# Two weight rows moved behind the later rwkv batches, and a block's input normalised ahead of the last context steps

## The chip, the cores and the metric

The kernel runs on one core of a Trainium2 chip. The metric is the device time of one execution in microseconds (us); less is better.

## The reference, cut to what matters

Two blocks run one after the other on a sequence of 512 tokens of width 1024. The first block (norm, projection, a gated linear recurrence beside dilated attention, output projection) gives `x`. The second block modulates its norms with six vectors that come from a conditioning vector, `mod = silu(c_2) @ w_ada_2 + b_ada_2`, cut into six pieces of 1024. Pieces 0 and 1 modulate the first norm, piece 2 scales the mixer's output, pieces 3 and 4 modulate the second norm, piece 5 scales the mixture of experts:

```python
p_l = modulate(x, norm1_g, mod[0], mod[1]) @ w_in      # 512 latent tokens
p_c = modulate(ctx, norm1_g, mod_c[0], mod_c[1]) @ w_in  # 256 context tokens
...
S_c, y_c = wkv_bidir(S0, *prep_c)      # rwkv over the context, both directions
_,   y_l = wkv_bidir(S_c, *prep_l)     # then over the latent tokens
...
x = x + mod[2] * mix
x = x + mod[5] * hier_moe(modulate(x, norm2_g, mod[3], mod[4]))
```

So the pieces 2 and 5 are needed late: one after the mixer, one inside the experts. The kernel calls the two rows `m2` and `m5`.

## The kernel before, in words

All is in single precision. A large product is split into a high and a low part of each operand and made of three matmuls (`mm3`, lines 311 to 313). A weight chunk of 512 KB is loaded into a raw buffer by SyncE's queue (`load_chunk`, line 298), and copied to its high part by ScalarE (line 305) and its low part by VectorE (line 306).

The program is written as one list of work. Which instruction each engine takes next is fixed when the kernel is built, by a planner that runs through an assumed timeline and, of the instructions that it takes to be ready, picks the one that stands earliest in the list. On the chip every engine, and every DMA queue, then runs its own list strictly in order. To put work into gaps, the list is woven by hand with Python generators: `step(n)` advances the generators of the modulation vectors in `fill` by n steps, and `cstep(n)` those of the context.

One step of `m2` or `m5` (`row_steps`) computes 256 columns of a row. SyncE's queue loads 256 bias values and two weight chunks of 512 KB; TensorE makes eight products of 32 x 256 (16 MATMUL records, line 384); ScalarE copies the sum out of PSUM (line 386); TensorE adds the four partial rows with one small product (two records, line 388); VectorE adds the bias (line 389), for `m2` also a factor (line 391); SyncE's queue stores 1 KB to DRAM (line 392). Four steps are a row, eight are both.

```python
r, b = (t2(name + z, w=256, tag="t1") for z in "rb")
...
p = ps(name + "p", "mm")
...
raw = load_chunk(w, v0 * 1024 + c * 256, kt=4, ..., nw=256, k0=4 * kh)
```

The buffers of a step, that is the two `t1` tiles, the two `mm` banks of PSUM and the raw buffers, belong to groups that the projections of the same stage use too. There are four raw buffers up to the end of the context and two during the rwkv batches; `mm` has three banks before and two after.

The order of the list around the change is this. First block's output, `mix`. Then the context's steps (`ctx_steps`): after a norm and two projections come the twelve steps of `rw_prep` for the context, which are two of low-rank inputs, two of low-rank outputs (line 772), four of keys and four of values (`vt`, lines 727 to 729 and 845); the second half of the keys is finished inside the first step of values (`key2`, lines 811 to 826). Then the four steps of `m2`. Then the second block's input: `norm_rows` (lines 424 to 427) and `mod_T`, which transposes `mix` in eight column blocks (line 436), scales each out of PSUM (lines 449 and 451) and splits it into high and low part (lines 453 and 454); the result is `h2`. Then the four steps of `m5`. Then the pools of weight buffers and of PSUM are closed and new ones are opened in their place, and the latent half begins: `rw_prep` over `h2` with 14 projections, woven with batches 0 to 3, which run the recurrence over the context, and with ten projections for gates. After it the batches 4 to 11 run the recurrence over the latent tokens. A batch loads its keys and decays (`kb`, `kr`, lines 1132 to 1136), makes products, sends a triangular matrix through DRAM (lines 1183 and 1187), inverts it with a long list of small VectorE instructions (`ph_s`, lines 1199 and 1201), sends it back through DRAM (lines 1204 and 1218) and updates the state (`ph_b`). Behind the batches in the list come the projections for queries, keys, values, pooling and the remaining gates of the latent tokens (`pt` and `pf` on TensorE); they need only `h2` and weights, so they run between the batches' instructions.

Of the kernel before, what the change touches and what calls it, by code (L numbers as in the profile page):

```python
# [186 lines left out]
def build(tc, A, out, dbg=None, upto=99):  # L187
    with ExitStack() as ctx:
        _build(ctx, tc, A, out, dbg, upto)


def _build(ctx, tc, A, out, dbg, upto):
# [61 lines left out]
    def t2(name, dt=F32, w=512, tag="t2"):  # L254
        return cur["bp"].tile([128, w], dt, tag=tag, name=name, bufs=NB[tag])
# [26 lines left out]
    def cc(name):  # L282
        g, o, w = _COFF[name]
        return csts[g][:, o:o + w]
# [67 lines left out]
    def step(n=1):  # L352

        while n and fill:
            try:
                next(fill[0])
                n -= 1
            except StopIteration:
                fill.pop(0)
# [98 lines left out]
    def hl(src, name, w=512):  # L458

        h = t2(name + "h", F32R, w)  # L460
        l = t2(name + "l", F32R, w)
        SC.activation(h, src, AF.Copy)
        V.tensor_tensor(l, src, h.bitcast(F32), ALU.subtract)
        return h, l
# [171 lines left out]


    yb = []
    MX = 4
    MS, MA = (0, 0, 0, 4), (3, 2)  # L640
    bias1 = cc("bias1")
    def att_scores(ft, e):

# [241 lines left out]
    def ctx_steps():  # L885

        xc = []
        for i in range(2):
            t = t2("xc%d" % i, w=1024, tag="t4")
            with tc.issue_after(ld1):  # L890
                SY.dma_start(t, A["ctx"][128 * i:128 * (i + 1), :])
            xc.append(t)
        hcH = bp.tile([128, 8, C], F32R, name="hcH")
        hcL = bp.tile([128, 8, C], F32R, name="hcL")
        norm_rows(xc, "hc")
        hc = mod_T(xc, gsc, sh2[:, 8:16], "hc", lambda f: (hcH[:, f], hcL[:, f]))
        yield
        kc = tok_tiles(W2, 1024, "kc", hc, 2)
        yield
        for i, t in enumerate(kc):  # L900
            qk_norm(t, "kcn")
            V.tensor_tensor(t.rearrange("p (h r) -> p h r", r=64), t.rearrange("p (h r) -> p h r", r=64),
                            qkg[:, None, 64:128].to_broadcast([128, 8, 64]), ALU.mult)
            dump("kc", t, 128 * i)
        for f, o in enumerate(to_feat(kc, "kcT", 2)):
            h, l = hl(o[:, :C], "kcs", C)
            spill_k(f, h, l, slice(512, 768))
        vc = tok_tiles(W2, 1536, "vc", hc, 2)
        for i in range(2):
            SY.dma_start(vcd2[:, i, :], vc[i])  # L910
        yield
        yield from rw_prep(hc, C, 0, False, "aux")

    NC = (2, 0, 99)
    cx = ctx_steps()

    def cstep(n=1):
        for _ in range(n):
            next(cx, None)
# [122 lines left out]
    for f in range(8):  # L1042
        src, g = (ya[f], vv("norm_rec")[:, f:f + 1]) if f < 4 else (yb[f - 4], vv("norm_att")[:, f - 4:f - 3])
        V.tensor_scalar(src, src, g, None, op0=ALU.mult)
        yhl.append(hl(src, "y%d" % f))
    cstep(NC[0])
    mix = [t2("mix%d" % i, w=1024, tag="t4") for i in range(4)]
    for cch in range(4):
        hh = halves(A["w_out"], 256 * cch)
        for i in range(4):  # L1050
# [8 lines left out]
            V.scalar_tensor_tensor(m, pa[:, 256:512], rb[:, i:i + 1], m, op0=ALU.mult, op1=ALU.add)  # L1059
    cstep(NC[1])  # L1060
    step(MS[2])
# [15 lines left out]

    cstep(NC[2])
    step(MS[3])
# [3 lines left out]
    cstep(99)  # L1083
    step(MX)

# [21 lines left out]
    def w1(name, shape=(4, 64), bufs=1, dt=F32):  # L1107
        p = rp if name == "AZ" else rpa if name in EARLY else rpb
        return p.tile([128] + list(shape), dt, tag=name, name=name, bufs=bufs)

    def bc(ap, sh):
        return ap.to_broadcast(sh)
# [65 lines left out]
    def ph_i(d, AMB, bi):  # L1178

        for e in range(2):  # L1180
            for i in range(2):
                r0 = 64 * e + 32 * i
                SY.dma_start(atD[bi][e, i].rearrange("q s t -> s q t"),
                             AMB[r0:r0 + 32, e, :, :, 32 * i:32 * i + 32].rearrange("p s f t -> p (s f) t"))
        LT = w1("LT", (32, 32), 2)
        for g in range(4):
            SY.dma_start(LT[32 * g:32 * g + 32].rearrange("p s t -> p (s t)"),
                         atD[bi].rearrange("e i q s t -> (e i q) (s t)"))
        return LT

    def ph_s(d, LT, bi):

        T = w1("Ti", (8, 32), 2)
        SY.dma_start(T.rearrange("p j t -> p (j t)"), A["tinit"])
        tmp = w1("Tm", (8, 32))
        for s in (range(31) if d == 0 else range(31, 0, -1)):
            js, ts_ = (slice(0, s // 4 + 1), slice(s + 1, 32)) if d == 0 else (slice(s // 4, 8), slice(0, s))
            nj, n = js.stop - js.start, ts_.stop - ts_.start
            V.tensor_tensor(tmp[:, :nj, :n], bc(LT[:, s, None, ts_], [128, nj, n]),  # L1199
                            bc(T[:, js, s:s + 1], [128, nj, n]), ALU.mult)  # L1200
            V.tensor_tensor(T[:, js, ts_], T[:, js, ts_], tmp[:, :nj, :n], ALU.add)  # L1201
        td = ttD[bi].rearrange("e i q (j g) t -> g (e i q) j t", g=4)
        for g in range(4):
            SY.dma_start(td[g], T[32 * g:32 * g + 32])
# [122 lines left out]
    def run_b():  # L1327
        n, sts = pend.pop(0)
        ph_b(*sts)
        if n == 3 and dbg is not None and "S_c" in dbg:  # L1330
            for d_ in range(2):
                for e, rows in par:
                    SY.dma_start(dbg["S_c"][128 * d_:128 * d_ + 128][rows, 256 * e:256 * e + 256],
                                 SI[d_, e][rows].rearrange("p a b -> p (a b)"))

    def batch(n):
        d, chs = batches[n]
        AMB = w1("AMB", (2, 2, 4, 192), 3)
        sts = {c - min(chs): ph_a(d, c, c - min(chs), AMB) for c in chs}
        LT = ph_i(d, AMB, n % 4)  # L1340
        while loops:
            ph_s(*loops.pop(0))
        loops.append((d, LT, n % 4))
        pend.append((n, (d, chs, sts, AMB, n % 4)))
        if len(pend) > 2:
            run_b()
# [42 lines left out]
        GP.memset(t, 0.0)  # L1389
    for n in range(4, 12):  # L1390
        batch(n)
    ph_s(*loops.pop(0))
    while pend:
        run_b()
# [744 lines left out]
```

## Time and profile before

| what | value |
|---|---|
| time, median of 3 runs | 1863.11 us (1859.43 to 1864.79) |
| the profiled execution's own time | 1868.35 us |
| its span in the profile | 1866.5 us |
| TensorE busy | 1715.4 us, 92% of the span |
| VectorE busy | 1068.7 us, 57% |
| ScalarE busy | 617.4 us, 33% |
| mean granted TensorE clock | 0.952 of full speed |

A share of the span is a mean over stages with different limits, so the rows below go stage by stage. Times in the rows are microseconds from the span's start. The 1.85 us between the span and the execution's own time lie outside the profile.

### The profile page before, as it was taken

To read this page: it belongs to the slowest core of one execution; us is meant where nothing else is said; L and a number is where in the kernel's file an instruction comes from. 1 tells how busy PE (TensorE), PEld (TensorE's weight loads), DVE (VectorE), ACT (ScalarE), POOL (GpSimd) and SP (SyncE) were. 2 spreads that over 40 slices of the span, in tenths; PEclk is the share of its full clock that TensorE was granted. 3 is DMA by queue.
4 is the path that set the end of the run, shared out by engine and by line. 5 is a ranking of instruction groups with operands and counts; after the bars stand their busy time and mean duration, and the time that the engine had idled before them with its cause. 6 is when DMAs were issued, how large, how long until landed. Compare 5 with 4: busy or idle time off the path is not lost.

```text
span 1866.5 us, 31358 instructions
## 1 busy us (share of the span) xinstructions
PE 1715.4 (92%) x12309; PEld 1216.4 (65%) x12310; DVE 1068.7 (57%) x2489; ACT 617.4 (33%) x1154; POOL 230.4 (12%) x254
## 2 busy tenths in 40 slices
PE   5899998977998899999999969989799999999998
PEld 3884577964665777888888846779644544444444
DVE  3545577374578856989888538865513333432332
ACT  4324555453443232344333324542311111111010
POOL 0110003001104102212200015100100001010100
PEclk8999999987898998999999989999899999999999
DMA  8335723467847555556654367628189999999997
GB/s 295 126 110 198 237 79 124 160 213 210 232 130 183 158 171 126 157 166 157 181 142 122 102 225 240 223 67 311 46 302 387 386 386 386 387 387 387 386 386 275
DMA packets 277744, 417.34 MB, mean 224 GB/s; under 512 B 105788, under 2 KB 128856, under 8 KB 277336
## 3 DMA queue, kind: packets, MB, share of 16 engines
q1 hardware_dynamic: 248696, 384.88, 61.7%
q10 hardware_dynamic: 25568, 16.78, 2.9%
q0 software_dynamic: 3328, 13.63, 2.6%
q8 instruction: 98, 1.61, 0.4%
q14 instruction: 54, 0.44, 0.1%
HBM read 371.70 MB, written 43.53 MB: 222 GB/s over the span
## 4 chain that ended last, share of the span: by engine, by line
PE 73%; DVE 11%; DMA 7%; ACT 3%; issue 3%; SPq 2%; POOL 1%; ACTq 0%; DVEq 0%; POOLq 0%
PE ped L1983 7%; PE peg L1944 6%; PE peu L1951 6%; PE pf L311 5%; PE pf L313 4%; PE pf L312 4%; PE pcb L2015 3%; PE po L1806 2%; PE pt L311 2%; PE pt L313 2%; PE pt L312 2%; PE pg L1917 2%; PE pg L1918 2%; DVE Tm L1199 1%; DMA kb<-kbD 1%
## 5 line engine op out<-in xcount | busy, mean ns | idle before, releaser
L306 DVE TENSOR_TENSOR wl<-wr,wh 128x1024 fp32r<-128x1024 f32 x125 | 153.5, 1228 | 65.0 <-ACT wh L305 63.4
L305 ACT ACTIVATE wh<-wr 128x1024 fp32r<-128x1024 f32 x125 | 131.8, 1056 | 171.5 <-PE pf L312 91.9
L311 PE MATMUL pf<-h2h,wh 128*128 128x512 f32 x344 | 144.5, 420 | 10.7 <-ACT wh L305 4.7
L312 PE MATMUL pf<-h2l,wh 128*128 128x512 f32 x344 | 142.4, 414 | 0.0
L313 PE MATMUL pf<-h2h,wl 128*128 128x512 f32 x344 | 141.2, 410 | 0.0
L1983 PE MATMUL ped<-wd,hid 128*64 128x512 f32 (+1 forms) x528 | 127.6, 585 | 0.7 <-ACT hid L1967 0.7
L1944 PE MATMUL peg<-wg,hTg 128*64 128x512 f32 x512 | 127.0, 597 | 0.0
L1951 PE MATMUL peu<-wu,hTg 128*64 128x512 f32 x512 | 125.1, 594 | 0.0
L2016 DVE TENSOR_TENSOR acc<-acc,pcb 128x512 f32<-128x512 f32 (+1 forms) x124 | 75.9, 665 | 47.0 <-PE pcb L2015 46.8
L1989 POOL TENSOR_TENSOR yl<-ey,yh 128x512 fp32r<-128x512 f32 x30 | 38.3, 1278 | 468.1 <-ACT yh L1988 468.1
L1199 DVE TENSOR_TENSOR Tm<-LT,Ti 128x60 f32<-128x60 f32 (+24 forms) x372 | 86.3, 232 | 14.0 <-DMA LT<-atD 5.3
L1201 DVE TENSOR_TENSOR Ti<-Ti,Tm 128x60 f32<-128x60 f32 (+24 forms) x372 | 82.2, 221 | 8.6
L1951 PEld LDWEIGHTS peu<-wu,hTg 128*64 128x64 f32 x512 | 43.8, 137 | 65.2 <-issue 62.8
L311 PEld LDWEIGHTS pf<-h2h,wh 128*128 128x128 f32 x344 | 67.5, 196 | 28.8 <-ACT wh L305 5.2
L1983 PEld LDWEIGHTS ped<-wd,hid 128*64 128x64 f32 x528 | 39.4, 136 | 71.4 <-issue 67.7
L1944 PEld LDWEIGHTS peg<-wg,hTg 128*64 128x64 f32 x512 | 41.8, 137 | 60.9 <-issue 58.1
L313 PEld LDWEIGHTS pf<-h2h,wl 128*128 128x128 f32 x344 | 66.8, 194 | 21.9 <-issue 5.6
L312 PEld LDWEIGHTS pf<-h2l,wh 128*128 128x128 f32 x344 | 67.3, 196 | 17.7 <-issue 3.0
L1988 ACT ACTIVATE yh<-ey 128x512 fp32r<-128x512 f32 x30 | 18.9, 630 | 166.7 <-DVE ey L1987 94.4
L1921 ACT ACTIVATE hTg<-pg,sh,gs 128x128 f32<-128x128 f32 x64 | 28.2, 456 | 121.7 <-PE peu L1951 55.4
L1924 DVE TENSOR_SCALAR hTg<-pg,gs,sh 128x128 f32<-128x128 f32 x64 | 25.3, 409 | 75.3 <-PE peu L1951 38.4
L311 PE MATMUL pt<-wh,h1h 128*128 128x256 f32 x192 | 56.4, 296 | 6.7 <-ACT q L547 4.3
(958 smaller groups left out, 4309.4 us busy)
## 6 DMA issues: line engine op xcount, KB each, us to landing
wg<-in_w_exp_gate_dram SPq DMA_DIRECT2D x64, 1024.0 KB
wu<-in_w_exp_up_dram SPq DMA_DIRECT2D x64, 1024.0 KB
wd<-in_w_exp_down_dram SPq DMA_DIRECT2D x62, 1024.0 KB
wr<-in_w_in_dram SPq DMA_DIRECT2D x97, 512.0 KB
kb<-kbD SPq DMA_DIRECT2D x24, 384.0 KB
wr<-in_w_out_dram SPq DMA_DIRECT2D x16, 512.0 KB
LT<-atD SPq DMA_DIRECT2D x48, 128.0 KB
thD<-mth ACTq DMA_DIRECT2D x24, 256.0 KB
```

The source lines that it names most:

```text
L305: SC.activation(hi, raw, AF.Copy)
L306: V.tensor_tensor(lo, raw, hi.bitcast(F32), ALU.subtract)
L311: PE.matmul(p, ah, bh, start=start, stop=False)
L312: PE.matmul(p, ah, bl, start=False, stop=False)
L313: PE.matmul(p, al, bh, start=False, stop=stop)
L1199: V.tensor_tensor(tmp[:, :nj, :n], bc(LT[:, s, None, ts_], [128, nj, n]), bc(T[:, js, s:s + 1], [128, nj, n]), ALU.mult)
L1201: V.tensor_tensor(T[:, js, ts_], T[:, js, ts_], tmp[:, :nj, :n], ALU.add)
L1944: mm = PE.matmul(pg[64 * a:64 * a + 64, :], hT[:, k, 64 * a:64 * a + 64], gp[a][k // 4][:, k % 4, :], start=(k == 0), stop=(k == 7), tile_ ...
L1951: PE.matmul(pu[64 * a:64 * a + 64, :], hT[:, k, 64 * a:64 * a + 64], up[a][k // 4][:, k % 4, :], start=(k == 0), stop=(k == 7), tile_posit ...
L1983: PE.matmul(pd[64 * a:64 * a + 64, :], hid[:, m * k + 64 * a:m * k + 64 * a + 64], dn[q][a][:, k, 0:q1 - q0], start=(k == 0), stop=(k == 3 ...
L2015: PE.matmul(p, ohT[R, 128 * i:128 * (i + 1)], yy[R, qs], start=(z == 0), stop=(z == len(parts) - 1))
L2016: V.tensor_tensor(acc[i][:, qs], acc[i][:, qs], p, ALU.add)
```

## The change

The context's steps ahead of the second block's input are cut from all twelve to nine: both low-rank pairs, the four keys, and the first value step with the second half of the keys. `norm_rows` and `mod_T` come next in the list, then the three remaining value steps. The eight steps of `m2` and `m5` are taken out of their two places around the second block's input, and one is put behind each of the batches 4 to 11.

```diff
     yb = []
-    MX = 4
-    MS, MA = (0, 0, 0, 4), (3, 2)
+    MX = 0
+    MS, MA = (0, 0, 0, 0), (3, 2)
     bias1 = cc("bias1")
...
-    NC = (2, 0, 99)
+    NC = (2, 0, 9)
     cx = ctx_steps()
...
     for n in range(4, 12):
         batch(n)
+        step(1)
     ph_s(*loops.pop(0))
```

`MS[3]` is the number of row steps ahead of `norm_rows` and `MX` that behind `mod_T`; `NC[2]` is the number of context steps ahead of `norm_rows`, and a `cstep(99)` behind `mod_T` takes what is left.

## Rows read from the trace of the kernel before

**Rows 1.** Stretches: busy us (instructions) by engine, granted clock, DMA share, GB/s.

```profile
128.00:218.00 90.00, 89.89 (x600) 39.42 (x600) 45.40 (x142) 42.26 (x121) 0.00 (x0) 1.00 0.67 228
392.00:434.00 42.00, 34.20 (x195) 28.28 (x195) 25.68 (x38) 24.32 (x42) 4.96 (x4) 0.88 0.51 133
434.00:469.00 35.00, 22.05 (x175) 8.76 (x175) 16.10 (x32) 12.75 (x26) 5.31 (x10) 0.77 0.82 261
700.00:1088.00 388.00, 368.57 (x4221) 313.41 (x4220) 307.94 (x973) 142.91 (x277) 61.63 (x94) 0.96 0.56 150
1082.00:1101.00 19.00, 3.13 (x34) 2.29 (x34) 3.04 (x8) 1.95 (x4) 0.92 (x1) 0.66 0.77 275
```

**Rows 2.** The chain of waits, 434 to 470: start, duration, what.

```profile
438.91 5.62 DMA m2w2r<-in_w_ada_dram
...
463.12 4.63 DMA wr<-in_w_in_dram
...
467.78 1.06 ACT wh L305
...
468.89 0.79 PE pf L311
```

**Rows 3.** Timeline of TensorE, 398 to 460: start, duration, what, idle before.

```profile
398.49 1.04 PE L436 MATMUL h2T<-cst,mix 128*128 128x128 f32 x8
...
432.44 0.28 PE L313 MATMUL pf<-hcH,wl 128*128 128x256 f32 x1
...
435.48 1.34 PE L384 MATMUL m2p<-m2w0r,st 128*32 128x256 f32 x16
...
452.69 0.59 PE L388 MATMUL m5q<-m5r,cst 128*1 128x256 f32 x2 [0.50 <-ACT m5r L386]
453.60 0.64 PE L384 MATMUL m5p<-m5w1r,st 128*32 128x256 f32 x8 [0.31 <-DMA m5w1r<-in_w_ada_dram]
...
457.44 1.08 PE L384 MATMUL m5p<-m5w2r,st 128*32 128x256 f32 x8 [0.37 <-DMA m5w2r<-in_w_ada_dram]
```

**Rows 4.** Timeline of SyncE's queue, the last spill of the context's keys.

```profile
436.44 1.44 SPq L778 DMA_DIRECT2D kbD<-tha  x2
```

**Rows 5.** Timeline of VectorE, 434 to 456.

```profile
434.07 0.53 DVE L825 TENSOR_SCALAR tha<-tha,ka 128x512 f32<-128x512 f32 x1
...
439.51 0.48 DVE L729 SCALAR_TENSOR_TENSOR vt<-pf,vec,vt 128x255 f32<-128x255 f32 x1
...
440.99 0.79 DVE L451 TENSOR_SCALAR h<-h2T,gs,sh 128x512 f32<-128x512 f32 x1
...
454.82 0.67 DVE L454 TENSOR_TENSOR h2l<-h,h2h 128x512 fp32r<-128x512 f32 x1
```

**Rows 6.** Groups by line, 434 to 469: count, busy us, mean ns, idle before.

```profile
L454 DVE TENSOR_TENSOR h2l<-h,h2h 128x512 fp32r<-128x512 f32 x8 | 5.2, 673 | 0.0
L453 ACT ACTIVATE h2h<-h 128x512 fp32r<-128x512 f32 x8 | 4.9, 627 | 1.7 <-DMA vTD<-vTs 1.7
L451 DVE TENSOR_SCALAR h<-h2T,gs,sh 128x512 f32<-128x512 f32 x4 | 3.2, 800 | 2.0 <-PE h2T L436 2.0
```

**Rows 7.** First and last of 20 like steps behind attention: ns, first and last start.

```profile
L336 PE MATMUL m2scp<-m2scw0r,st x16: 379/379/403, 128.0 to 128.7; 128*32 128x256 f32 x16
...
L336 PE MATMUL m3shp<-m3shw3r,st x16: 379/391/403, 214.7 to 217.2; 128*32 128x256 f32 x16
```

**Rows 8.** The chain of waits, two `kb` loads.

```profile
488.86 6.61 DMA kb<-kbD
...
534.37 3.52 DMA kb<-kbD
```

**Rows 9.** Stretches of those two loads, columns as in the first group.

```profile
488.80:495.80 7.00, 7.00 (x41) 4.88 (x40) 0.24 (x2) 1.94 (x5) 0.10 (x1) 1.00 0.77 206
534.30:538.00 3.70, 3.70 (x17) 2.98 (x16) 2.49 (x8) 1.72 (x5) 0.61 (x2) 1.00 0.65 200
```

**Rows 10.** Waits of SyncE's queue, 700 to 1090: us in total, times, longest.

```profile
SPq L1321 <- ACT yt L1320: 50.9, 9, 23.8
```

## The prediction

> **What bounds the kernel now.** I read the table of stretches first [rows 1], then the chain of waits through the place where work is taken out [rows 2], and then the lists of the single engines there [rows 3 to 6]. The reader is to see two very different stretches. From 434 to 469, where the rows `m2` and `m5` and the second block's input lie, TensorE shows 22.05 us of records in 35 us, at a granted clock of 0.77, that is partly at the lower of its two levels, while the DMA engines are at 0.82 and move 261 GB/s. From 700 to 1088, where the batches 4 to 11 run, TensorE is busy for 368.57 of 388 us at a clock of 0.96, and the DMA engines are at 0.56.
>
> The chain of waits says what the first stretch waits for: weight chunks of the row steps, 5.62 us for one of them, then the first chunk of the latent half, issued at 463.12, which lands 4.63 us later, and its split [rows 2]. The first latent product starts at 468.89. The last product of the context started at 432.44 [rows 3]. So for 36.45 us TensorE does no projection: sixteen chunks of 512 KB, 8.4 MB, pass through raw buffers, and the latent half's first chunk stands behind them in SyncE's queue. That wait ends last in this stretch, and it is a wait for transfers, not for an engine.
>
> **Part 1: the rows leave the stretch.** The step from 36.45 us to what must remain goes by what is late next. Without the rows, the first latent product needs a chunk, its split, and the first column block of `h2`.
>
> The chunk: SyncE's queue still has the context's spills to issue, the last at 436.44 for 1.44 us, so it is free at 437.88 [rows 4]. If the load goes out then, it lands after the 4.63 us measured for the same load, at 442.51; ScalarE's 1.06 us of split end at 443.57 [rows 2], and the first product starts there, as it follows the split's end within a microsecond today. It gains 468.89 - 443.6 = 25.3 us. If the planner issues the load ahead of the spills, the chunk is no limit and the product can start where the context's products end, at about 433: a gain of at most 36 us.
>
> The input: the first two blocks' transposes run at 398.49 [rows 3], but VectorE scales the first block only at 440.99, behind the last value step's instruction at 439.51, and writes the last low part at 455.49 [rows 5]. With three value steps put behind it in the list, its place is behind the end of the second half of the keys, at 434.60 [rows 5]. Its work is 8 x 0.673 + 4 x 0.800 = 8.6 us on VectorE, and 8 x 0.627 = 5.0 us on ScalarE plus the other four scalings [rows 6], so some 9 us if it runs without the rows' instructions between, and it is done at about 444. A projection takes the eight blocks in order, so it can start with the first. The other bound is that the tail stays as it is, first block at 441, last at 455.5: then the first projection can't run through before that, starts in effect at about 450, and gains 19 us. I take 25.3, since chunk and input agree on it, with 19 and 36 as bounds.
>
> **Part 2: three value steps behind the input.** They are the same instructions in another place. Their evacuations, two instructions of 0.48 us on VectorE for each [rows 5], fall beside the first latent projection instead of before the input. TensorE has 42 - 34.2 = 7.8 us without a record from 392 to 434 [rows 1], where the remaining 24 transposes can go; at 1.04 us for eight [rows 3] they are 3.1 us. I cost this edit at nothing; if that cover is gone, the transposes stay where they are and cost their 3.1 us, which lies inside the bounds above. The values' spills come later in their queue by that, and only a batch that updates the state waits for them.
>
> **Part 3: the rows come back behind the batches.** Per step TensorE needs its 16 records, 1.34 us when nothing holds them up, of which the last one's 0.38 us [rows 7] overlap what follows, and 0.59 us for the two that add the partial rows [rows 3]: 0.96 + 0.59 = 1.55 us, and 8 x 1.55 = 12.4 us. ScalarE and VectorE get one or two copies or sums of 256 columns a step, on engines that are busy for 142.91 and 307.94 of the 388 us, and the DMA engines have 44% free there [rows 1]. SyncE's queue gets three loads and a store a step. I cost these at nothing; what it costs if the queue gives no cover is the first rival.
>
> The lower bound is nothing: TensorE lacks 388 - 368.57 = 19.4 us of being busy there, and behind the last batch, where its output goes out to DRAM and in again, 19 - 3.1 = 15.9 us are empty that displaced projections could fill [rows 1]. The upper bound is the pace of the steps today, where they run alone: from 453.60 to 457.44, 3.84 us a step [rows 3], 30.7 us for eight. The nearest row for steps that lie behind other work is attention: 20 like steps ran from 128 to 218 [rows 7], and TensorE was busy for 89.89 of those 90 us [rows 1]. Steps cost their own TensorE time there and no idle time. So I take 12.4 us.
>
> **The sum.** The profiled execution took 1868.35 us, span 1866.5 and 1.85 around it, which is 5.2 us above the median of the three runs. 1868.35 - 25.3 + 12.4 = 1855.4; against the median, 1863.1 - 12.9 = 1850.2 us. Everything after the latent half moves forward with it: the experts' weights at the end are loaded at a rate that the change doesn't touch.
>
> **A rule that speaks against it.** In the trace two loads of `kb` that stand on the chain took 6.61 and 3.52 us [rows 8], the slower one in a stretch where the DMA engines were at 0.77, the other at 0.65 [rows 9]. The Trainium skill, "DMA: Bandwidth & Descriptors", section "Issuing engines are not separate DMA queues", says that all DMAs run on the same 16 engines and interleave, whoever started them. By that rule the batches' small transfers would get slower while a row's chunks are in flight, and the two rows above agree with it in direction. What it would cost is the first rival.
>
> **The rivals.**
> *Late transfers on the batches' path (slower).* The eight steps issue 16 chunks, 8 bias loads and 8 stores on the queue that also issues `kb`, `kr` and the triangular matrices' way through DRAM. A store waits at its head for VectorE's sum, and a chunk for a raw buffer; behind it stand the next batch's loads, and ScalarE, VectorE and TensorE wait for those. Such waits exist: 50.9 us over nine stores of the batches, the longest 23.8 us [rows 10]. Priced at the difference of the two `kb` loads, 3.1 us for each of eight batches, it is 24.7 us: 1863.1 - 25.3 + 12.4 + 24.7 = 1875 us. It makes the change slower from (25.3 - 12.4 + 5.6) / 8 = 2.3 us a batch. Against it: two batches are always in hand ahead of the one that updates the state, and the steps need nothing of the batch that they follow, so they may run early.
> *The input holds the latent half (no difference).* If the tail of `h2` stays at 441 to 455.5, 19 us are gained; if the steps also take 2 us each rather than 1.55, because they hold both `mm` banks while ScalarE and VectorE are busy, 16 to 19 us are lost again: 1860 to 1863 us. For it speaks that the first block lay in PSUM for some 41 us, from 399.5 to 440.99 [rows 3, 5], so something other than its input held it.
> *The rows are hidden (faster still).* If they fill the idle time in the batches and the empty wait behind them, the second term is nothing: 1863.1 - 25.3 = 1838 us, and with the product's start at 433, 1827. For it speak the 19.4 and 15.9 us; against it that the first is made of pieces of a microsecond or two.
>
> **How the numbers follow.** I give the forecast 0.48, late transfers 0.18, no difference 0.14, hidden rows 0.20. The forecast's own range, with the gain from 19 to 29 and the rows from 5 to 16 us, is 1843 to 1858. No change can be told from a measurement here within 0.3%, 5.6 us, so faster is the forecast and the hidden rows, 0.68; the same 0.14; slower 0.18. The range reaches from 1835, which leaves out a third of the hidden rows' case, to 1868, which leaves out most of the late transfers' case: about 2 in 10 together.
>
> **What would show it.** Right: the first latent product near 443 instead of 468.89 and no line 384 before it; the first block of `h2` scaled before 437; the rows' line 384 only after about 670, its steps 1 to 2 us of TensorE each, with the batches' end near 1088 - 25 + 12 = 1075. Wrong: a latent start later than 455, with VectorE or ScalarE of `mod_T` as its last wait; steps in a run with TensorE idle for chunks between them and the projections for queries starting late; or batches that wait for `kb`, the triangular matrices or the store of a row. Any of the last adds to the stretch of the batches, which I have taken as bounded by TensorE; if it is bounded by VectorE's list, the rows are free and the time is under 1843.

## The result, and the profile after

The changed kernel takes 1878.1 us (median of 9 runs, 1871.36 to 1883.98) against 1864.79 us (9 runs) before: the ratio is 1.0071, with an interval of 1.0055 to 1.0087. It is slower by some 13 us, where 1850 and a faster kernel were forecast. The profiled execution has a span of 1876.4 us. The two profiled executions differ ahead of all that the change moves in the list: the first block's output projection starts at 325.0 us before and at 321.6 after. So 3.4 us of each lead below are not the change's, and each delay is larger by as much.

The front part gained about what was forecast. These stretches have the columns of [rows 1]:

```profile
434.00:446.00 12.00, 2.43 (x13) 1.48 (x13) 10.28 (x18) 8.52 (x15) 3.84 (x9) 0.61 0.71 213
446.00:469.00 23.00, 23.00 (x101) 15.98 (x102) 13.29 (x32) 9.62 (x20) 4.26 (x11) 0.91 0.77 226
700.00:1088.00 388.00, 357.92 (x3949) 299.19 (x3949) 285.80 (x907) 131.00 (x257) 50.56 (x82) 0.88 0.58 161
1063.00:1082.00 19.00, 19.00 (x81) 14.79 (x80) 8.67 (x10) 5.22 (x7) 0.14 (x2) 1.00 0.61 196
```

From 446 on TensorE is saturated, where it was waiting for row chunks before. The first latent product and the first scaling of `h2`, from the timelines of TensorE and VectorE:

```profile
439.04 0.66 PE L845 MATMUL vTp<-cst,vt 128*128 128x128 f32 x2 [3.51 <-DVE vt L729]
443.30 0.66 PE L845 MATMUL vTp<-cst,vt 128*128 128x128 f32 x2 [3.60 <-DVE vt L729]
445.98 0.66 PE L845 MATMUL vTp<-cst,vt 128*128 128x128 f32 x2 [2.03 <-DVE vt L729]
446.29 0.78 PE L311 MATMUL pf<-h2h,wh 128*128 128x512 f32 x1
```
```profile
430.42 0.80 DVE L451 TENSOR_SCALAR h<-h2T,gs,sh 128x512 f32<-128x512 f32 x1
```

446.29 instead of 468.89 is a lead of 22.6 us, 19.2 of them the change's. At the latent half's gate (the `tanh` of line 875) it is 700.3 - 667.8 = 32.5 us, 29.1 of them the change's. The loss lies behind that. The projections' first products (line 311), by stretch: busy us and count on TensorE, the same for weight loads, granted clock, DMA share, GB/s. Before:

```profile
680.00:725.00 45.00, 9.27 (x24) 4.93 (x25) 0.86 0.40 123
725.00:770.00 45.00, 14.34 (x40) 8.30 (x40) 0.95 0.66 160
770.00:812.00 42.00, 13.32 (x42) 7.90 (x42) 1.00 0.59 152
```

After:

```profile
680.00:725.00 45.00, 0.00 (x0) 0.00 (x0) 0.68 0.71 177
725.00:770.00 45.00, 0.00 (x0) 0.00 (x0) 0.58 0.43 115
770.00:812.00 42.00, 0.00 (x0) 0.00 (x0) 0.74 0.48 146
812.00:850.00 38.00, 9.93 (x31) 6.67 (x31) 0.91 0.45 130
```

For 132 us no projection runs at all: 106 such products of line 311 in the kernel before, none after. The query projections start at 812.5 instead of 717.2, right behind the last row step. In their place stand the batches' small products and the eight row steps, whose line 384 spreads from 682.9 to 806.7, some 16 us a step. The batches don't get faster by it. Their last `yt` is at 1060.0 instead of 1087.7, a lead of 27.7 us, but it was 32.5 us at the gate: from there they take 392.2 us instead of 387.4, though no projection stands among them for 132 us. VectorE waits for their triangular matrices in that stretch (680 to 810; us in total, times, longest), 11.2 us where it was 2.0 us before (680 to 812):

```profile
DVE Tm L1199 <- DMA LT<-atD: 11.2, 3, 4.5
```

The projections are left over. They fill the wait behind the batches that was empty (19.00 us busy of 19 from 1063 to 1082, 3.13 of 19 in [rows 1]), and still the last gate is at 1139.2 instead of 1118.8. Half of these 20.4 us come back behind the gate: products of the latent attention that stood behind it before now run ahead of it, and from the gate to the experts TensorE has 197.15 us of records instead of 206.32. The experts start 10.4 us late, at 1363.0 instead of 1352.6, and so does everything behind. With the 3.4 us from the front that is 13.8 us, about the 13.3 us between the medians.

Why a step takes 16 us shows where the last two meet. TensorE, then SyncE's queue (start, duration, what):

```profile
779.88 1.43 PE L384 MATMUL m5p<-m5w2r,st 128*32 128x256 f32 x5
...
799.71 0.64 PE L384 MATMUL m5p<-m5w2r,st 128*32 128x256 f32 x8
```
```profile
778.63 1.05 SPq L298 DMA_DIRECT2D m5w2r<-in_w_ada_dram  x1
...
783.98 0.35 SPq L298 DMA_DIRECT2D m5w3r<-in_w_ada_dram  x1
793.73 0.34 SPq L1134 DMA_DIRECT2D kr<-kkD  x1
...
800.41 0.34 SPq L298 DMA_DIRECT2D m5w3r<-in_w_ada_dram  x1
...
803.71 1.44 SPq L298 DMA_DIRECT2D wr<-in_w_in_dram  x1
```

The second half of step 7 runs 21 us after its chunk was issued, because batch work stands before it in TensorE's list. Only then is its raw buffer free for the last chunk (800.41), and the first chunk for the projections comes behind that (803.71). The queue itself also stood from 784 to 793.73 for a batch's `kr`, which waits for VectorE to let go of its buffer; the waits of the queue, 680 to 810 (us in total, times, longest), show this as the largest:

```profile
SPq L1134 <- DVE AR L1154: 15.0, 3, 9.4
SPq L298 <- PE m2p L384: 9.5, 2, 8.3
```

### The profile page after: what moved, and what is told of

It is laid out like the page before. It is cut to its first block, busy times and chain, and to the rows that moved or that the text cites. A ratio compares the mean times of both kernels' runs of the same rounds, so it can differ in the third digit from the quotient of the medians.

```text
span 1876.4 us, 31396 instructions
## 1 busy us (share of the span) xinstructions
PE 1732.9 (92%) x12309; PEld 1230.6 (66%) x12310; DVE 1070.4 (57%) x2489; ACT 617.5 (33%) x1154; POOL 226.5 (12%) x254
## 4 chain that ended last, share of the span: by engine, by line
PE 71%; DVE 13%; DMA 8%; issue 2%; ACT 2%; SPq 2%; POOL 1%; DVEq 0%; ACTq 0%; POOLq 0%
PE ped L1984 6%; PE peg L1945 6%; PE peu L1952 6%; PE pf L311 4%; PE pf L312 4%; PE pf L313 4%; PE pcb L2016 3%; PE po L1807 2%; PE pt L311 2%; PE pt L313 2%; PE pt L312 2%; PE pg L1918 2%; PE pW L1287 2%; DVE wl L306 2%; PE pg L1919 2%
## 5 line engine op out<-in xcount | busy, mean ns | idle before, releaser
L1201 DVE TENSOR_TENSOR Ti<-Ti,Tm 128x60 f32<-128x60 f32 (+24 forms) x372 | 86.0, 231 | 8.9
L1925 DVE TENSOR_SCALAR hTg<-pg,gs,sh 128x128 f32<-128x128 f32 x64 | 25.3, 408 | 75.5 <-PE peu L1952 38.4
```

## The experiments

Ratios and medians are against the kernel before, run on the same chip beside them; its median was 1861.8 to 1864.1 us.

### The two halves of the change, and the rows elsewhere

**The input's new place alone**, rows where they were:

```diff
-    MX = 0
-    MS, MA = (0, 0, 0, 0), (3, 2)
+    MX = 4
+    MS, MA = (0, 0, 0, 4), (3, 2)
...
         batch(n)
-        step(1)
```

> One part alone: nine context steps ahead of the second block's input, the rows where they were before the change. Theories A, B and C agree: the row chunks again stand ahead of the latent half's first chunk, so the first latent product stays within 460 to 470 and the time within 1858 to 1868 us. If the input's place gave the lead by itself, it would be under 1850 us.

Measured: 1851.28 us, 0.9931 [0.9914, 0.9947]. With nine context steps ahead of them, the four steps of `m2` run at 403.8 to 426.6, in the context's gaps, and the first latent product is at 461.75. So 1864.06 - 1851.28 = 12.8 us of gain come without taking the rows out at all. The first product stands where the theories had it, the time lies under their 1858 to 1868.

**The rows' new place alone**, all context steps ahead of the input:

```diff
-    NC = (2, 0, 9)
+    NC = (2, 0, 99)
```

> The other part alone: all context steps ahead of the input as before the change, the rows behind the batches. If the rows' leaving gives the lead, the first latent product starts at 445 to 452, with 17 to 24 us gained there, and the loss behind the batches is the same as in the changed kernel, about 45 us: 1885 to 1893 us. If the place of the input gives the lead, the first product stays near 465 and the time is above 1895 us.

Measured: 1877.7 us, 1.0073 [1.0049, 1.0097], the same as both together and under the 1885 to 1893 expected: first latent product at 445.0, query products only from 810.4. So the rows' leaving gives the lead at the first latent product by itself, and the input's new place adds nothing that the time shows once the rows are gone. The loss belongs to the rows.

**The rows behind the batches' end**, where `FM` brings them up in the pooling's part of the list:

```diff
         batch(n)
-        step(1)
```

> The changed kernel without the step behind each batch; the eight row steps then run where the list still has steps left, in the pooling projections, behind the projections for queries, keys and values. Theory A (the sixteen row chunks stand in the list ahead of the latent projections' chunks and use the same two raw buffers, so TensorE has no projection from about 680 to 812): the lead of 32 us that the changed kernel has at the start of the batches stays, less some 12 us of TensorE work for the rows at the end, so 1840 to 1850 us, first latent query product near 690. Theory B (row transfers and row instructions burden whatever they lie beside): the rows cost as much beside the pooling, 1865 to 1880 us. Theory C (the two mm banks of PSUM or the t1 tiles that a step holds keep the projections away): the pooling projections use the same banks, so at least half the loss comes back, 1855 to 1870 us.

Measured: 1860.86 us, 0.9986 [0.9966, 1.0006]. The query products start at 681.8, the batches end at 1040.8, 47 us ahead of before; then the steps run from 980 to 1084 and hold up the pooling, TensorE is busy for 34.24 of the 50 us from 1050 to 1100, and the last gate is at 1119.6, as before. The lead is lost in another place. The time is in the range of theory C, the start of the query products where theory A had it; what the steps hold back there was not taken apart.

### What holds the projections back

**Their own raw buffers** (256 KB pieces through the two `tp` tiles):

```diff
-                raw = load_chunk(w, ..., kt=4, name=name + "w%d" % c, nw=256, k0=4 * kh)
                 for g in range(4):
+                    if g % 2 == 0:
+                        rt = t2(name + "w", w=544, tag="tp")
...
```

> The changed kernel with the rows' chunks loaded in halves of 256 KB into the two buffers that the pooling uses later, instead of the projections' raw buffers; place, number of bytes, PSUM banks and t1 tiles as in the changed kernel. Theory A: latent query products start near 690 instead of 812, and the time falls to 1845 to 1860 us. Theory B: same bytes, same instructions, no change, 1875 to 1885 us. Theory C: the banks and tiles are as before, no change, 1873 to 1882 us, query products still after 790.

Measured: 1901.09 us, 1.0206 [1.0183, 1.023]: worse, which none of the three theories had. The one that the shared raw buffers alone hold the projections falls here. The first query chunk was split by 661.66, ScalarE's last line 305 before the stop, and still its product waited for the last row step. From the timelines of ScalarE and TensorE:

```profile
660.60 1.06 ACT L305 ACTIVATE wh<-wr 128x1024 fp32r<-128x1024 f32 x1 [1.70 <-PE pf L312]
```
```profile
844.31 0.59 PE L391 MATMUL m5q<-m5r,cst 128*1 128x256 f32 x2 [0.48 <-ACT m5r L389]
844.83 0.39 PE L311 MATMUL pt<-wh,h2h 128*128 128x256 f32 x1
```

**Their sums in other banks of PSUM**, raw buffers shared:

```diff
-            p = ps(name + "p", "mm")
+            p = ps(name + "p", "aux")
...
-            q = ps(name + "q", "mm")
+            q = ps(name + "q", "aux")
```

> The changed kernel, but the partial sums of a row step and their total are taken from the three aux banks of PSUM instead of the two mm banks that the projections use; chunks still pass through the shared raw buffers. Theory banks (banks are given out in the order of the list, so the query projections that stand behind all eight steps get no mm bank before the last step has one): the first query product moves from 812 to before 725; as chunks of later steps still stand ahead of the projections' chunks in the raw buffers, only the chunks that are already split can be used early, so the time falls by 5 to 15 us, to 1863 to 1873. Theory raw buffers (refuted alone by the run with its own raw tiles, but kept here): first query product stays at 800 or later, time 1873 to 1885. Theory loads on the batches' path: no difference, 1873 to 1885.

Measured: 1921.08 us, 1.0312 [1.0275, 1.0348]. Query products start only at 937.0: the raw buffers hold them now, and the steps take some 33 us each. The theory of the raw buffers had the late start, none of the three the time. The `aux` banks are those of the batches' own updates; that sharing them sets this pace was not tried by itself.

**Both** of these edits:

> The changed kernel with both: the steps' sums in the aux banks, and their weights as 256 KB pieces through the two large tp tiles instead of the projections' raw buffers. A step then holds nothing that the projections use. Theory banks: the query products start at 680 to 720 and fill the batches as in the kernel before, and the gain in front is kept: 1843 to 1860. Theory turns (the steps' pieces among the batches' instructions set the pace by themselves, not what they hold): the batches end later than 1060 and the time stays at 1873 to 1900. Theory loads (the 8.4 MB slow the batches' own transfers): batches' end later than 1065, 1865 to 1880.

Measured: 1897.6 us, 1.0208 [1.0174, 1.0242]. The time is in the range of the theory of turns, but its sign did not come: the batches end at 1002.0, not after 1060. Now the first sixteen query products start at 685.4, and from 725 to 900 there is nothing of line 311. What they wait for is the third group that a step takes from: the `t1` tiles. The first user of `t1` behind the rows is the copy `sw` for the queries' tables, and the first sum `dq` is taken out of PSUM right behind the last row's copy. VectorE's `sw` (duration, first and last start), then ScalarE's timeline:

```profile
L1410 DVE COPY sw<-qkg x1: 222/222/222, 916.3 to 916.3; 128x128 f32<-128x128 f32 x1
```
```profile
916.72 0.36 ACT L389 ACTIVATE m5r<-m5p 128x256 f32<-128x256 f32 x1
916.99 0.37 ACT L1456 ACTIVATE dq<-pt 128x256 f32<-128x256 f32 x1
```

**Nothing shared with the next projections:** sums in `aux`, row and bias in one `tp` tile, weights in 128 KB pieces through the halves of the other:

```diff
-            r, b = (t2(name + z, w=256, tag="t1") for z in "rb")
+            r, b = ROW[0][:, 0:256], ROW[0][:, 256:512]
...
+                    raw = ROW[1][:, 256 * (g % 2):256 * (g % 2) + 256]
+                    SY.dma_start(raw, w[2 * (4 * v0 + c) + kh][:, 256 * g:256 * g + 256])
```

> The changed kernel, its row steps with nothing that the projections use: sums in the aux banks, row and bias in one of the two large tp tiles, weights in pieces of 128 KB through the halves of the other. Theory list order (every shared group of buffers, the raw buffers, the two mm banks and the six t1 tiles, is handed out in the order of the list; with raw buffers and banks taken away, the queries' first sum still waited from 691 until 917 for its t1 tile, behind the last row step): query products run from 690 on without a gap and fill the batches; the gain in front is kept, and the rows cost 0 to 15 us: 1840 to 1862. Theory that the loads or the turns of the steps among the batches' instructions cost the time in any case: query products may start early, but the batches end after 1080 or the projections run at half their pace, 1870 to 1900.

Measured: 1889.02 us, 1.0133 [1.0097, 1.0169]. The start came as the theory of the list's order said. Time and batches' end (1111.2) came as the other theory said, that loads or turns cost the time in any case. `sw` is at 696.1 and the first query sum at 697.1:

```profile
L1409 DVE COPY sw<-qkg x1: 214/214/214, 696.1 to 696.1; 128x128 f32<-128x128 f32 x1
```

But the `tp` tiles belong to the pooling, which comes later, and the steps last until 1040. ScalarE's timeline shows the same picture one group further:

```profile
1039.83 0.38 ACT L387 ACTIVATE row<-m5p 128x256 f32<-128x256 f32 x1 [1.26 <-PE m5p L385]
1040.11 0.59 ACT L1510 ACTIVATE plu<-pf 128x512 f32<-128x512 f32 x1
```

### What the loads cost, and what the holding

**Without the sixteen loads**, banks and `t1` shared:

```diff
-                raw = load_chunk(w, ..., kt=4, name=name + "w%d" % c, nw=256, k0=4 * kh)
-                    PE.matmul(p[...], st[:, 4 * kh + g, :], raw[:, g, :],
+                    PE.matmul(p[...], st[:, 4 * kh + g, :], H2[4 * kh + g][0].bitcast(F32)[:, 0:256],
```

> The changed kernel without the sixteen loads of the row steps' chunks: their products read blocks of h2 instead, so the contents of the rows m2 and m5 are not the weights' and the output differs. Sums stay in the mm banks. Theory banks: the steps keep their pace of 10 us or more, as each stands at its place in the list behind its batch, and the query products still start only when the last step has its banks, after 780: 1865 to 1880. Theory loads: steps shrink to 2 to 4 us of elapsed time each, the query products start before 725, and the time falls to 1838 to 1855.

**The same with nothing held** (sums in `aux`, row and bias in a `tp` tile):

> The same without the loads of the rows' weights: products read blocks of h2, so the contents of the rows m2 and m5 are not the weights' and the output differs; sums in the aux banks, row and bias in a tp tile. Beside the run without loads that shared banks and t1 tiles (1856), it prices what holding these two costs alone. Theory list order: query products from 690, 1832 to 1850, at least 6 us under 1856. Theory loads alone (banks and tiles cost nothing once the steps don't wait for transfers): the same as 1856 within 4 us.

Measured: 1856.08 us, 0.9978 [0.9952, 1.0004], and 1831.05 us, 0.983 [0.9797, 0.9863]. Without loads the steps pass in 66 us (681 to 747) and the query products start at 752.6; both figures lie between the two theories of this run. With nothing held that the projections take next they start at 686.4, and the steps take from 696 to 970 to pass, which no longer shows in the time. Line 311 in that run:

```profile
680.00:725.00 45.00, 10.43 (x32) 6.87 (x32) 0.91 0.59 139
725.00:770.00 45.00, 13.95 (x42) 7.89 (x42) 1.00 0.65 173
770.00:812.00 42.00, 11.18 (x33) 6.02 (x32) 1.00 0.52 152
```

107 products where the changed kernel had none. Taken away in this order, the loads are worth 1878.1 - 1856.1 = 22 us and the holding that is left without them 25 us. The two do not simply add. With the holding taken away first and the loads kept, which is the run with nothing shared, the time is 1889.0, and leaving the loads out gains 1889.0 - 1831.1 = 58 us from there. That run passes its weights in 128 KB pieces through one small tile, so the 58 us are not the price of the transfers alone.

**All eight steps ahead of batch 4**, and **four behind batch 4, four behind batch 5**, everything shared:

```diff
+    step(8)
     for n in range(4, 12):
         batch(n)
-        step(1)
```

> All eight row steps in a run ahead of batch 4 in the list, behind the latent half's gate, instead of one behind each of the batches 4 to 11; banks and raw buffers shared as in the changed kernel. Theory banks: the banks are free for the query products as soon as the steps are through, at the 3.8 us a step of the kernel before after some 31 us, so the first query product comes at 700 to 735, and the time is 1850 to 1866. Theory turns or loads: the eight steps cost the same wherever they stand, first query product after 780, 1872 to 1890.

> The changed kernel with four row steps behind batch 4 and four behind batch 5 in the list instead of one behind each of eight batches; everything shared as in the changed kernel. Theory list order: the time follows the moment when the last row step lets go of its t1 tiles and the queries' first sum is taken out of PSUM. From the runs so far: let go at 692, 755, 760, 825 and 848 us gave 1831, 1858, 1856, 1878 and 1901, some 0.4 us for each us. Here between the run with all eight ahead of batch 4 (755) and the changed kernel (825): 760 to 800, and 1858 to 1872. Theory that the price is of the transfers alone: the same as the changed kernel, 1873 to 1885.

Measured: 1857.99 us, 0.9981 [0.9961, 1.0001], and 1862.69 us, 1.0009 [0.9987, 1.003]. Both times lie where the theory of the banks, or of the list's order, put them. With all eight ahead of batch 4 the query products start at 747.1, though, later than the 700 to 735 expected: in a run there the steps take some 9 us each, not 3.8. The first query sum is taken out at 754.8 and 762.4. In order of that moment:

| run | first `dq`, us | time, us |
|---|---|---|
| nothing held, no loads | 692.5 | 1831.1 |
| all first | 754.8 | 1858.0 |
| no loads | 760.3 | 1856.1 |
| four by four | 762.4 | 1862.7 |
| the change | 825.0 | 1878.1 |
| own raw buffers | 848.0 | 1901.1 |
| other banks and own raw buffers | 917.0 | 1897.6 |
| other banks | 941.5 | 1921.1 |

That is (1921.1 - 1831.1) / (941.5 - 692.5) = 0.36 us for each us of delay. It is a trend over different kernels, not a law; the rows' new place alone (820.9, 1877.7) lies on it, the run with nothing shared (697.1, 1889.0) lies off it: its pooling waited until 1040, and its batches ended at 1111.2, against 1052.9 without the loads. So does the run with the rows behind the batches' end (687.8, 1860.9), whose loss comes later.

### The row that the forecast used

**m2 in the first block's attention**, m5 ahead of the input, and **all eight there**, with `(0, 0, 0, 0), (4, 3)`; the input's new place kept, no step behind the batches:

```diff
-    MS, MA = (0, 0, 0, 0), (3, 2)
+    MS, MA = (0, 0, 0, 4), (4, 2)
```

> The input's new place kept; the four steps of m2 are woven into the first block's attention (four steps after each even head instead of three), the four of m5 stand behind the nine context steps ahead of the input, none behind the batches. Theory that a step among saturated work costs its own TensorE time where what it holds is not shared with work in waiting: attention grows by 4 x 1.55 = 6 us, the m5 steps run in the context's gaps at 400 to 430 plus 6, the first latent product stands 10 to 16 us earlier relative to that than in the run with the input's place alone (461.8): 1836 to 1850. Theory that what counts is only the rows' transfers wherever they are: no better than 1851.

> All eight row steps in the first block's attention (four after each even head, three after each odd one), the input's new place kept, none behind the batches. Theory own TensorE time: attention grows by 8 x 1.55 = 12 us and the rest is the lead of 25 us: 1845 to 1857, and the end of attention is 10 to 16 us later than before. Theory that steps come at a pace of transfers or buffers there too: attention grows by 20 us or more, 1858 to 1875.

Measured: 1866.49 us, 1.0013 [0.9995, 1.0031], and 1876.65 us, 1.0076 [1.0051, 1.01]. The output projection starts at 321.6 in the changed kernel, 330.9 with four steps more, 344.9 with eight (ns, first and last start):

```profile
L311 PE MATMUL pa<-wh,y0h x16: 278/280/282, 321.6 to 363.9; 128*128 128x256 f32 x16
```
```profile
L311 PE MATMUL pa<-wh,y0h x16: 277/280/415, 330.9 to 373.4; 128*128 128x256 f32 x16
```
```profile
L311 PE MATMUL pa<-wh,y0h x16: 277/280/282, 344.9 to 387.1; 128*128 128x256 f32 x16
```

Counted from the first step in the attention (at 122.9, 122.7 and 125.2) that is 9.5 / 4 = 2.4 and 21.0 / 8 = 2.6 us a step, not 1.55. But it is not the price of a step among saturated work. The attention itself takes as long as ever, 78.8 us from the first to the last start of its products of line 676, and the added steps run behind it. The kernel before, then the run with all eight and the first of its steps (ns, first and last start):

```profile
L676 PE MATMUL po<-aPT,v x64: 272/458/644, 135.3 to 214.1; 128*64 128x512 f32 x16, 128*64 128x384 f32 x16, 128*64 128x256 f32 x16, 128*64 128x128 f32 x16
```
```profile
L676 PE MATMUL po<-aPT,v x64: 272/458/643, 132.5 to 211.3; 128*64 128x512 f32 x16, 128*64 128x384 f32 x16, 128*64 128x256 f32 x16, 128*64 128x128 f32 x16
L384 PE MATMUL m2p<-m2w0r,st x16: 379/379/403, 212.3 to 213.9; 128*32 128x256 f32 x16
```

There they stand almost alone, some 3 us a step: TensorE has 15.89 us of records in the 25.1 us from 212.3 to 237.4, at a DMA share of 0.92. That is the sign of the theory of a pace of transfers or buffers; the time lies just over its range. Both times lie over the ranges of the theories of own TensorE time, but what a step more costs inside a saturated stretch was not measured. With four steps more the first latent product stood at 462.8; counted from the output projection that is 8.7 us earlier than with the input's place alone, less than the 10 to 16 us expected.

### Versions with rows ahead of the input, and half of them late

**All eight ahead of the input**, behind nine context steps and, with `NC = (2, 0, 10)`, behind ten; no step behind the batches:

```diff
-    MS, MA = (0, 0, 0, 0), (3, 2)
+    MS, MA = (0, 0, 0, 8), (3, 2)
```

> The input's new place with all eight row steps ahead of it in the list, behind the nine context steps, instead of four ahead and four behind; none behind the batches. With the four of m5 behind the input, the first latent product stood at 461.8, as the chunks of m5 came from 444 to 455. Theory transfers (sixteen chunks have to come through before the first latent chunk wherever they stand): the rows move into the context's gaps, first latent product at 450 to 462, 1840 to 1853. Theory that the context's last steps then wait for the rows' raw buffers: first latent product later than 462, 1853 to 1865.

> As the run with all eight row steps ahead of the input, with ten context steps ahead of them instead of nine. Theory transfers: no difference to nine within 4 us. Theory context's waits: the fewer context steps stand behind the rows, the less they wait; faster than nine by 2 to 8 us.

Measured: 1856.24 us, 0.9974 [0.9953, 0.9994], first latent product at 463.8; and 1872.16 us, 1.0051 [1.0031, 1.0072], at 471.9. The first is as the theory had it that the context's last steps wait for the rows' raw buffers. Ten steps are worse by 16 us, not the same or better, which neither theory had: `h2` is then split from 433.2 instead of 426.0.

**m2 ahead of the input, m5 ahead of batch 4**, or, without the `step(4)`, **in the pooling's part of the list**:

```diff
-    MS, MA = (0, 0, 0, 0), (3, 2)
+    MS, MA = (0, 0, 0, 4), (3, 2)
...
+    step(4)
     for n in range(4, 12):
         batch(n)
-        step(1)
```

> The input's new place, m2's four steps ahead of it in the context's gaps as in the run with the input's place alone, and m5's four steps in a run ahead of batch 4 instead of behind the input. Theory list order: the first latent product comes at 445 to 452 instead of 461.8, a lead of 10 to 16 us; the four steps let go at about 700 to 720, so the queries' first sum is late by no more than 10 to 25 us, which costs 0.35 to 0.4 us for each us, 4 to 10 us: 1838 to 1852, at or a little under the 1851 of the input's place alone. Theory transfers: the 4.2 MB cost the same wherever they stand: 1848 to 1856.

> The same with m5's four steps not ahead of batch 4 but behind the batches, in the pooling's part of the list (two in each of the first two pieces). With all eight there the lead of 47 us at the batches' end was lost at 13 to 15 us a step between 980 and 1082. Theory list order and pace: half the steps lose half of it, some 25 us of a lead of some 35: 1846 to 1856. Theory that the empty wait behind the batches takes up four steps: 1835 to 1846.

Measured: 1851.21 us, 0.9912 [0.9884, 0.994], and 1840.11 us, 0.9879 [0.985, 0.9908], the fastest version beside the one that leaves the loads out. In the first, the first latent product is at 456.3, later than expected, and the time lies in the ranges of both theories; three of its ten runs took 1833 to 1839 us and the others 1849 or more, so that the ratio of the medians would be 0.994. In the second, the query products start at 684.2; the pooling's stretch takes up four steps (993.0 to 1037.6), which it did not do with eight. TensorE from 961 to the end of the batches' wait, first with four steps there, then with all eight:

```profile
961.00:1076.00 115.00, 106.31 (x1121) 83.10 (x1120) 68.41 (x183) 36.27 (x64) 3.77 (x12) 0.97 0.53 168
```
```profile
961.00:1091.00 130.00, 104.18 (x1044) 72.04 (x1042) 62.24 (x153) 35.42 (x63) 3.77 (x12) 0.89 0.55 175
```

About the same busy time, 15 us apart. It came out under the 1846 to 1856 expected for half the loss, in the range of the theory that the empty wait behind the batches takes up four steps.

## Why the prediction was wrong

**Part 1 was right in size.** It gave 25.3 us with bounds of 19 and 36; 19.2 us were measured at the first product and 29.1 us at the end of the latent half, when the 3.4 us from the front are taken off. What ended last was neither chunk nor input: the first chunk's high part was ready at 439.9 and the last block of `h2` at 440.1, and the product follows the value steps' last transpose at 445.98 on TensorE's list. The prediction credited the gain to the rows leaving, and their new place alone gives that lead (445.0). The input's place alone gains 12.8 us without that, so the two gains overlap and do not add.

**Part 2 was not at nothing.** The value steps' evacuations did not fall beside the first latent projection but ahead of it: TensorE waits 3.51, 3.60 and 2.03 us for them, and the product comes some 6 us after chunk and input are ready. That lies in the 12 us from 434 to 446 that were counted to part 1, and inside its bounds.

**Part 3 failed**: "Steps cost their own TensorE time there and no idle time. So I take 12.4 us." With part 1 at its 25.3 us, the term measured 1878.1 - (1864.8 - 25.3) = 38.6 us, outside its bounds of 0 to 30.7. Three things were wrong in it. First, the row it was taken from: attention was busy for 89.89 of 90 us [rows 1] with twenty steps woven in, but that says nothing of what a step more costs: steps added there ran behind the attention, at 2.4 to 2.6 us each. Second, the upper bound was the pace of steps that run alone, 3.84 us [rows 3]; behind batches a step took 16 us, since its halves stand among the batches' instructions in three in-order lists. Third, and the largest: the steps' own time was priced, and not what they hold meanwhile. ScalarE, VectorE and SyncE's queue were put at nothing, and the buffers had no term; only the rival of no difference names the two `mm` banks, at 2 us a step. The shared groups (`t1`, `mm`, raw) stood in the kernel's description, and each is handed out in the order of the list, ahead of projections that stand behind all eight steps. With loads and holding taken away, the 1831.1 us are no more than the 1864.8 - 25.3 = 1839.5 us of the front's gain alone: no TensorE time of the rows shows in it. That is in the 1827 to 1838 of the third rival, but in a kernel that does not load the rows' weights.

**The late transfers' rival** gave 1875 us, near the time measured, which is in part luck. Its mechanism took place in part: from the gate to the last `yt` the batches took 392.2 us, against 387.4 before and 379.0 with only the sixteen loads left out, and VectorE waited for their triangular matrices. But the larger loss is not in it: the rows waited in their turn behind the batches' entries in SyncE's queue and in TensorE's list, and the projections behind the rows. The Trainium skill, "DMA: Bandwidth & Descriptors", section "Issuing engines are not separate DMA queues", which had been weighed for it, says that all DMAs interleave on the same engines. The changed kernel's trace does not show a load slowed by that: two loads of `kb` on its chain of waits, from 680 to 812, took 5.94 and 3.55 us, against 6.61 and 3.52 in [rows 8]. The run with nothing shared with the next projections may: with projections and loads side by side its batches ended at 1111.2, without the loads at 1052.9. The `aux` banks, which its steps held while they waited for chunks, can have done the same; the two were not told apart.

**What would show it wrong** was named: steps in a run with TensorE idle between them and query projections that start late. That sign came, but the prediction had given it no price and no chance of its own. Batches that wait for the triangular matrices came too.

The Trainium skill, "Perfetto Trace Analysis", section "Optimization Strategy", says that gaps repeating for a stretch on the engine that should be saturated can mean too little SBUF or PSUM for the next tile to be allocated. The trace agrees in kind: 106.26 of 132 us busy from 680 to 812 and no projection among them. Here it was not the size of a group but the order in which it was handed out; the same kernel with other places for the steps' tiles had 107 products there.

What stays open: how the price of the loads, 22 us or 58 by the order in which things are taken away, divides between the queue's order, the raw buffers and the transfers themselves. A run with its loads and with buffers and banks for the steps that nothing else ever uses was not made, nor one with the loads in another engine's queue, so that the cost of the transfers alone is not measured.

## What to carry to other kernels

Before moving work behind other work, list every rotating group that it takes from, and who stands next in the list for each; a filler step costs not its busy time alone, but also the time for which it keeps back what the next in the list needs, from its first tile to its last release. In the run without loads, a step that held only what nobody wanted next took over 30 us to pass and cost nothing that the time shows. Taking away one of several shared groups can make things worse, as the next one takes over. And look where an added step really runs: woven into the list of a stretch that is busy at 100%, the steps here ran behind it, so its busy share gave no price for them.

## What the hardware showed unexpectedly

The busy share of TensorE hid part of the loss. From 680 to 812 it is 106.26 of 132 us, against 124.51 before, though 106 products of line 311 and as many of lines 312 and 313 are missing. From 725 to 770 the changed kernel's TensorE was busy for 36.04 of 45 us at a granted clock of 0.58, near the lower of its two levels, where the kernel before had 0.95. Eight products of the batches (`pW`) took 2.08 us at 791.61, after 2.50 us of idle time, where the granted clock was 0.51 over 2.5 us. They took 1.16 us in the run with own raw buffers, where the granted clock of the 2 us around them was 1.00:

```profile
791.61 2.08 PE L1287 MATMUL pW<-AMB,XV 128*128 128x128 f32 x8 [2.50 <-ACT WW L1297]
```
```profile
839.69 1.16 PE L1290 MATMUL pW<-AMB,XV 128*128 128x128 f32 x8
```

So the same small products have longer records at the lower clock, and the busy share fell less than the work did: a product of line 1162 took 386 ns in the mean from 680 to 812, and 313 ns before. The projections' absence does not make the clock fall at every place: the run with own raw buffers has none around 839.69 either.
